# Attention of a two-layer trunk on one core: the turned weights and the values of two heads issued together, value columns of four heads in one matmul, and the lower parts of the first turned blocks in row order

## The chip, the cores and the metric

The kernel runs on one core of a Trainium2 chip. The metric is device time in microseconds. Three runs of the kernel before took 1935.15, 1935.57 and 1936.12 us; their median, 1935.57 us, is the time before. One more execution was profiled, and every row of a profile below is from such an execution.

## What is computed

A trunk of two layers over 256 rows of 2048 columns, all in float32. The first layer mixes rows with a convolution module, the second with latent attention over 16 heads; each is followed by a squared-ReLU MLP, and an RMS norm stands ahead of each part and at the end. What the change touches is the attention:

```python
down = h @ w_in
c_q, c_kv, k_pe = jnp.split(down, [Q_LORA_RANK, Q_LORA_RANK + KV_LORA_RANK], axis=-1)
q = (rms_norm(c_q, q_norm_g) @ w_q_up).reshape(B, S, N_HEADS, QK_NOPE_DIM + QK_ROPE_DIM)
...
kv = (rms_norm(c_kv, kv_norm_g) @ w_kv_up).reshape(B, S, N_HEADS, QK_NOPE_DIM + V_HEAD_DIM)
k_nope, v = jnp.split(kv, [QK_NOPE_DIM], axis=-1)
...
s = (jnp.einsum('bqhd,bkhd->bhqk', qn, k_nope)
     + jnp.einsum('bqhr,bkr->bhqk', qp, k_pe)).astype(jnp.float32) * scale
s = jnp.where(mask[None, None], s, -jnp.inf)
p = jax.nn.softmax(s, axis=-1).astype(v.dtype)
return jnp.einsum('bhqk,bkhd->bqhd', p, v)
...
return o @ w_o
```

The latent vectors have 512 columns; a head has 128 key columns, 64 rotary columns and 128 value columns. In the weight `w_kv_up` the 128 key columns and the 128 value columns of a head lie side by side, head after head.

## The kernel before

Products in float32 are made of two parts. A weight block comes in by DMA (`raw`, three buffers), ScalarE rounds it to its upper part (`hi`, line 169), VectorE subtracts to get the lower part (`lo`, line 173), six buffers of each. `mm3` (lines 202 to 204) then issues three matmuls for one product: upper by upper, lower by upper, upper by lower. The data side is split in the same way, by `hi_part` (208) and `lo_part` (213, or 215 with a scale). Only turns (transposes by an identity matrix) and the product of softmax weights and values run in plain float32; the trace lists a plain float32 matmul as two rows.

PSUM has eight banks. During the MLP all eight are `acc`; in the attention six are `acc` and two are `tr`, each kind used in rotation.

At the end of the first layer's MLP, `Sums.plain` calls `prepare` for the column blocks 0 and 1 of the new rows. Each `prepare` turns four 128-column blocks in two calls of `to_T`, two blocks to a PSUM bank. ScalarE takes the upper parts from the bank. VectorE's lower parts follow at once for the first call; for the second they are put in the list `rest`, which the next call with `rest` runs (or, at the end, the caller). The attention's first product reads these blocks, and its banks are those that the MLP gave up.

The attention works in groups of four heads (`HG = 4`). What a group needs is a list of pieces: `qp_piece` (rotary columns of a row half), `qn_piece` (a head's query, twelve matmuls of 256 columns), and `kv_piece`, eight to a group: for each pair of heads two pieces that make a head's keys (twelve matmuls of 256 columns) and two that make the values of both heads for a row half (line 1540 ff., again twelve matmuls, the moving operand being two runs of 128 value columns). The weight of a pair is one unit and one DMA of 1 MB (`kv_unit`). `start_unit` and `prefetch` start the split of the unit two places ahead and the load of the unit three further on. In the loop over heads the pieces of the group that comes next stand between the steps of the heads of this one; in the last group they are pieces of the output product (`o_piece`). One head runs:

```python
scores(h)
piece(todo.pop(0))
weights(h)
prefetch(1)
piece(todo.pop(0))
if h > 0:
    weights_turn(h - 1)
if i > 1 and g + 1 < NG:
    qp_turn(g + 1, i - 2)
if h > 1:
    values(h - 2)
```

`scores` makes ten matmuls into an `acc` bank, VectorE takes the row maxima (1640, 1641), ScalarE the exponentials (1643); `weights` divides by the sums on VectorE (1650, 1653) into `pr`. `weights_turn` turns the three 128 x 128 blocks of `pr` into a `tr` bank (1659) and ScalarE copies them to `pT` (1661). `qp_turn` turns the rotary parts of two heads of the next group into a `tr` bank (1597) and ScalarE copies them twice (1606, 1607). `values` multiplies `pT` with `vv` (1668, 1669) into an `acc` bank, which is split into `oh` and `ol` (208, 213). Everything from the down projection on is under `tc.manual_schedule()`: each engine runs its instructions in the order written. The number of pieces per head is 3, 2, 2, 2 in group 0, 4, 4, 3, 3 in groups 1 and 2, and 3 each in group 3.

Of the kernel before, what the change touches and what calls it, by code (L numbers as in the profile page):

```python
# [78 lines left out]
def trunk_kernel(  # L79
# [59 lines left out]
    def nm(s):  # L139
        uid[0] += 1  # L140
        return f"{s}_{uid[0]}"
# [233 lines left out]
    def residual_stage(last, gain, r_scale=None, raw=None, by_steps=()):  # L375
# [18 lines left out]
        def prepare(n, only=None, half=None, out=None, rest=None):  # L394
            sl = columns(n, half)
            if last:
                if n in by_steps:
                    step()
                    steps.extend(turn_block(n, gain, raw))
                elif gain is not None:  # L400
                    for j in range(2):
                        to_T(xs, 4 * n + 2 * j, xh, xl, gain, rest if j == 1 else None)
# [961 lines left out]
    with ExitStack() as cx:  # L1364
# [34 lines left out]
        def kv_unit(g, i):  # L1399
            unit(("kvu", g, i), [rows(mla_w_kv_up[0], 0, NJ, (g * HG + 2 * i) * (DN + DV), 2 * (DN + DV))],  # L1400
                 [P, NJ, 2 * (DN + DV)])
# [8 lines left out]
        for g in range(NG):  # L1410
            if g == 0:
                kv_unit(g, 0)
                kv_unit(g, 1)
                q_units(g)
            else:
                q_units(g)
                kv_unit(g, 0)
                kv_unit(g, 1)
# [90 lines left out]
        kTs, vvs, qTs, qps, qpAs = {}, {}, {}, {}, {}  # L1509
# [8 lines left out]
        def kv_piece(g, i, c):  # L1518

            key = ("kvu", g, i)  # L1520
            if i == 0 and c == 0:
                kTs[g] = parts_tile("kT")
                vvs[g] = gp[0].tile([P, T, HG * DV], F32, tag="vv", name=nm("vv"))
            if c % 2 == 0:
                start_unit(key, c // 2)
            po = acc_tile()
            if c < 2:
                o = po[:, :S]
                ns = slice(c * (DN + DV), c * (DN + DV) + DN)
                for j in range(NJ):  # L1530
                    wh, wl = w_at(key, j)
                    nc.tensor.matmul(o, wh[:, ns], kvh[:, j, :], start=j == 0, stop=False)  # L1532
                    nc.tensor.matmul(o, wh[:, ns], kvl[:, j, :], start=False, stop=False)  # L1533
                    nc.tensor.matmul(o, wl[:, ns], kvh[:, j, :], start=False, stop=j == NJ - 1)  # L1534
                in_parts(o, kTs[g], 2 * i + c)
            else:
                t = c - 2
                ts = slice(t * P, (t + 1) * P)
                o = po[:, : 2 * DV].rearrange("p (h n) -> p h n", h=2)
                for j in range(NJ):  # L1540
                    wh, wl = (a.rearrange("p (h n) -> p h n", h=2)[:, :, DN:] for a in w_at(key, j))
                    mm3(o, kvh[:, j, ts], kvl[:, j, ts], wh, wl, j == 0, j == NJ - 1)
                nc.vector.tensor_copy(vvs[g][:, t, 2 * i * DV : 2 * (i + 1) * DV], po[:, : 2 * DV])
# [65 lines left out]
        def kv_work(g):  # L1609
            return [lambda i=i, c=c: kv_piece(g, i, c) for i in range(HG // 2) for c in range(4)]  # L1610
# [14 lines left out]
        def scores(h):  # L1625
# [5 lines left out]
            pr = prs[h] = at2.tile([P, 3 * P], F32, tag="pr", name=nm("pr"))  # L1631
# [46 lines left out]
        def o_piece(k):  # L1678
# [5 lines left out]
            for b in range(2):  # L1684
                bs = slice(b * NB, (b + 1) * NB)
                for t in range(T):
                    mm3(ps_o[b][t], oh_kt(k, t), ol_kt(k, t), wh[:, bs], wl[:, bs], k == 0, k == H - 1)

        with tc.manual_schedule():
# [95 lines left out]
            for g in range(NG):  # L1785
                for i in range(HG):
# [11 lines left out]
                    if h > 0:  # L1798
                        weights_turn(h - 1)
                    if i > 1 and g + 1 < NG:  # L1800
                        qp_turn(g + 1, i - 2)
                    if h > 1:
                        values(h - 2)
# [115 lines left out]
```

## Time and profile before

| what | value |
|---|---|
| median of three runs (lowest to highest) | 1935.57 us (1935.15 to 1936.12) |
| profiled execution, its own time | 1935.27 us |
| its span in the trace | 1933.5 us |
| granted TensorE clock, mean over the span | 0.999 |
| PE, VectorE, ScalarE busy, share of the span | 99%, 82%, 57% |
| attention, first scores to last values | 1063.9 to 1191.2 us of the span |

A row of the timeline gives the start in us from the start of the span, the duration in us, engine, line of the kernel, operation, tiles as out<-in, shape, how many instructions were merged, and in brackets the idle time ahead of it with what ended it. Matmuls are pipelined: one starts before the one ahead of it has ended, so that the cost of one in a row of many is the distance between two starts, not the duration in its row. A row with "issue" or a releaser in brackets is where an engine stood still.

### The profile page before, as it was taken

The page shows a single profiled execution, that of the slowest core. Times are in us where ns is not written, and L with a number is a line of the kernel's source. Part 1 is how long each engine was busy: PE and PEld are TensorE (multiplying, and loading weights), DVE is VectorE, ACT ScalarE, POOL GpSimd, SP SyncE. Part 2 cuts the span into 40 slices and gives each one's busy share as a digit, 9 for nine tenths or more (in the row PEclk, how much of TensorE's full clock was granted, in tenths as well). Part 3 has the DMA queues.
Part 4 walks back from the last instruction along what each step waited for, and adds up shares of the span by engine and source line. Part 5 has one row for each costly group of instructions (what it writes and reads, how often), then busy time and mean ns, then how long its engine had stood idle before and what let it go on. Part 6 is the DMA issues. An engine that isn't in the chain of part 4 may idle for free.

```text
span 1933.5 us, 28599 instructions
## 1 busy us (share of the span) xinstructions
PE 1919.0 (99%) x10805; PEld 1684.2 (87%) x10805; DVE 1592.3 (82%) x2464; ACT 1095.5 (57%) x1634; POOL 249.0 (13%) x208
## 2 busy tenths in 40 slices
PE   8999999999999999999999999999999999999998
PEld 8999888888888888888899998888888888888886
DVE  7999988877989777799976766877789887678898
ACT  5667755554555555555586655555555554455554
POOL 6999200000010100000001420000000010000000
PEclk9999999999999999999999999999999999999999
DMA  7766456665585866555665445465546686665674
GB/s 230 214 184 188 153 192 205 192 195 176 177 253 190 262 199 186 192 174 196 218 188 161 142 133 191 157 217 185 187 163 224 214 251 219 191 196 175 231 220 148
DMA packets 217756, 375.50 MB, mean 194 GB/s; under 512 B 16009, under 2 KB 91025, under 8 KB 217361
## 3 DMA queue, kind: packets, MB, share of 16 engines
q1 hardware_dynamic: 211968, 363.28, 58.2%
q0 software_dynamic: 4320, 7.87, 2.2%
q10 hardware_dynamic: 1328, 2.52, 0.4%
q8 instruction: 84, 1.38, 0.3%
q14 instruction: 56, 0.45, 0.1%
HBM read 363.68 MB, written 2.10 MB: 189 GB/s over the span
## 4 chain that ended last, share of the span: by engine, by line
PE 96%; DVE 2%; issue 0%; DMA 0%; ACT 0%; ACTq 0%; DVEq 0%
PE acc L650 24%; PE acc L202 15%; PE acc L204 15%; PE acc L203 15%; PE acc L651 13%; PE acc L818 8%; PE acc L1281 2%; DVE sum L905 1%; DMA xs<-in_x 0%; PE acc L1532 0%; PE acc L1555 0%; PE acc L1557 0%; PE acc L1556 0%; PE acc L1534 0%; PE acc L1533 0%
## 5 line engine op out<-in xcount | busy, mean ns | idle before, releaser
L173 DVE TENSOR_TENSOR lo<-raw,hi 128x1024 fp32r<-128x1024 f32 (+2 forms) x509 | 601.7, 1197 | 231.6 <-ACT hi L169 227.8
L169 ACT ACTIVATE hi<-raw 128x1024 fp32r<-128x1024 f32 (+2 forms) x574 | 583.9, 1036 | 358.4 <-PE acc L650 196.6
L650 PE MATMUL acc<-xt,hi 128*128 128x512 f32 x2048 | 710.5, 390 | 0.0
L651 PE MATMUL acc<-xt,lo 128*128 128x256 f32 x2048 | 577.5, 282 | 0.0
L650 PEld LDWEIGHTS acc<-xt,hi 128*128 128x128 f32 x2048 | 384.4, 188 | 80.6
L651 PEld LDWEIGHTS acc<-xt,lo 128*128 128x128 f32 x2048 | 387.1, 189 | 0.2
L494 ACT ACTIVATE hi<-raw 128x1024 fp32r<-128x1024 f32 x248 | 228.8, 949 | 234.8 <-DVE raw L502 137.6
L495 DVE TENSOR_TENSOR lo<-raw,hi 128x1024 fp32r<-128x1024 f32 x248 | 264.0, 1087 | 31.9 <-ACT hi L494 27.9
L202 PE MATMUL acc<-hi,sh 128*128 128x512 f32 x514 | 200.1, 389 | 0.0
L204 PE MATMUL acc<-lo,sh 128*128 128x512 f32 x514 | 200.1, 389 | 0.0
L202 PE MATMUL acc<-hi,gh 128*128 128x512 f32 (+1 forms) x516 | 200.0, 388 | 0.0
L203 PE MATMUL acc<-hi,gl 128*128 128x512 f32 (+1 forms) x516 | 199.9, 387 | 0.0
L204 PE MATMUL acc<-lo,gh 128*128 128x512 f32 (+1 forms) x516 | 199.9, 387 | 0.0
L818 PE MATMUL acc<-xt,hi 128*128 128x256 f32 x1024 | 180.1, 281 | 0.3 <-ACT b L1100 0.2
L203 PE MATMUL acc<-hi,sl 128*128 128x512 f32 x450 | 175.1, 389 | 0.0
L575 POOL DMA_DIRECT2D xs<-v x30 | 26.4, 972 | 1138.2 <-DVE lo L173 703.9
L905 DVE SCALAR_TENSOR_TENSOR sum<-ub,w_dw,sum 128x256 f32<-128x256 f32 x409 | 164.4, 484 | 3.5 <-ACT sum L875 3.0
L173 POOL TENSOR_TENSOR lo<-raw,hi 128x1024 fp32r<-128x1024 f32 x65 | 155.1, 2410 | 17.3 <-ACT hi L169 17.3
L818 PEld LDWEIGHTS acc<-xt,hi 128*128 128x128 f32 x1024 | 154.5, 188 | 1.1 <-ACT xt L1084 0.6
L818 PE MATMUL acc<-xt,lo 128*128 128x256 f32 x512 | 139.2, 279 | 0.0
L204 PEld LDWEIGHTS acc<-lo,sh 128*128 128x128 f32 x514 | 96.5, 188 | 20.5 <-DVE lo L495 0.3
L204 PEld LDWEIGHTS acc<-lo,gh 128*128 128x128 f32 x516 | 96.9, 188 | 19.9
(311 smaller groups left out, 2563.1 us busy)
## 6 DMA issues: line engine op xcount, KB each, us to landing
raw<-in_mlp_w SPq DMA_DIRECT2D x255, 1024.0 KB, 5.4
raw<-in_conv_w_pw SPq DMA_DIRECT2D x62, 512.0 KB, 5.0
raw<-in_conv_w_pw SPq DMA_DIRECT2D x16, 1024.0 KB, 5.0
raw<-in_mla_w_o SPq DMA_DIRECT2D x16, 1024.0 KB, 5.3
raw<-in_mla_w_kv_up SPq DMA_DIRECT2D x8, 1024.0 KB, 5.3
xs<-v POOLq DMA_DIRECT2D x30, 256.0 KB, 7.7
raw<-in_mla_w_in SPq DMA_DIRECT2D x8, 576.0 KB, 4.6
raw<-in_mla_w_in SPq DMA_DIRECT2D x4, 1024.0 KB
```

The lines of the kernel that those rows point to most:

```text
L169: nc.scalar.activation(hi, raw[:, js, :], AF.Copy)
L173: eng.tensor_tensor(lo, raw, hi.bitcast(F32), op=ALU.subtract)
L202: nc.tensor.matmul(ps, sh, mh, start=start, stop=False)
L203: nc.tensor.matmul(ps, sl, mh, start=False, stop=False)
L204: nc.tensor.matmul(ps, sh, ml, start=False, stop=stop)
L494: nc.scalar.activation(hi, src, AF.Copy)
L495: nc.vector.tensor_tensor(lo, src, hi.bitcast(F32), op=ALU.subtract)
L650: nc.tensor.matmul(ps[b], wh[:, bs], xhl(k), start=k == 0, stop=False)
L651: nc.tensor.matmul(ps[b][:, :S], wl[:, bs], xh(k), start=False, stop=k == KC - 1)
L818: nc.tensor.matmul(pss[c][b][:, :S], w[i][:, bs], (xh, xl)[j](k), start=k == i + j == 0, stop=end and k == k0 + nk - 1 and (i, j) == terms ...
L905: nc.vector.scalar_tensor_tensor(out=out, in0=ubs[c][:, w : w + S], scalar=tap(c, w), in1=base, op0=ALU.mult, op1=ALU.add)
L1281: nc.tensor.matmul(ps2[b][t], x_kt(k, t), w[:, bs], start=k == g == i == 0, stop=k == KC - 1 and i == len(group) - 1,)
```

## The change

It has three parts.

1. `prepare`: before the first `to_T` of a column block, the list `rest` is emptied. The lower parts of blocks 2 and 3 then come ahead of those of 4 and 5. (Blocks are counted in 128 columns; this acts at one place, the end of the first MLP, since elsewhere `rest` is absent or empty.)
2. The units of `w_kv_up`: instead of two units of two heads with keys and values, a group has one unit with the key columns of four heads and one with the value columns of four heads. Each is loaded by four DMAs of 256 KB, in runs of 128 columns (512 bytes) where there were runs of 512 columns. A key piece is as before. A value piece now makes the values of four heads for a row half, with a moving operand of 512 columns; it is cut into two halves of six matmuls that add into one bank, and one copy of 512 columns ends it. A group has still eight pieces: four of keys, then four halves of values.
3. The order of turns and values: `plain_work` takes the place of the three calls in the loop. At an even head from 4 on it issues values(h - 4), weights_turn(h - 2), perhaps one qp_turn, values(h - 3), weights_turn(h - 1); at an odd head nothing, but for heads 1 and 15. `qp_turn(g, 1)` moves from the last head of a group to the first of the next. `pr` has a third buffer.

```diff
@@ prepare
                 elif gain is not None:
+                    while rest:
+                        rest.pop(0)()
                     for j in range(2):
                         to_T(xs, 4 * n + 2 * j, xh, xl, gain, rest if j == 1 else None)
@@ units
-        def kv_unit(g, i):
-            unit(("kvu", g, i), [rows(mla_w_kv_up[0], 0, NJ, (g * HG + 2 * i) * (DN + DV), 2 * (DN + DV))],
-                 [P, NJ, 2 * (DN + DV)])
+        wkv4 = mla_w_kv_up[0].rearrange("(j p) (h n) -> p j h n", p=P, n=DN + DV)
+
+        def kv_units(g):
+            hs = slice(g * HG, (g + 1) * HG)
+            for kind, ns in (("k", slice(0, DN)), ("v", slice(DN, DN + DV))):
+                unit((kind, g), [wkv4[:, j : j + 1, hs, ns] for j in range(NJ)], [P, NJ, HG * DN])
@@ pieces
+        def k_piece(g, i):
+            key = ("k", g)
...
+            if i % 2 == 0:
+                start_unit(key, i // 2)
+            o = acc_tile()[:, :S]
+            ns = slice(i * DN, (i + 1) * DN)
+            for j in range(NJ):
+                wh, wl = w_at(key, j)
+                nc.tensor.matmul(o, wh[:, ns], kvh[:, j, :], start=j == 0, stop=False)
+                nc.tensor.matmul(o, wh[:, ns], kvl[:, j, :], start=False, stop=False)
+                nc.tensor.matmul(o, wl[:, ns], kvh[:, j, :], start=False, stop=j == NJ - 1)
+            in_parts(o, kTs[g], i)
+
+        def v_piece(g, t, half):
+            key = ("v", g)
+            if half == 0:
+                start_unit(key, t)
+                vos[g, t] = acc_tile()
+            o, ts = vos[g, t], slice(t * P, (t + 1) * P)
+            for j in range(half * NJ // 2, (half + 1) * NJ // 2):
+                mm3(o, kvh[:, j, ts], kvl[:, j, ts], *w_at(key, j), j == 0, j == NJ - 1)
+            if half == 1:
+                if t == 0:
+                    vvs[g] = gp[0].tile([P, T, HG * DV], F32, tag="vv", name=nm("vv"))
+                nc.vector.tensor_copy(vvs[g][:, t, :], o)
@@ kv_work
-            return [lambda i=i, c=c: kv_piece(g, i, c) for i in range(HG // 2) for c in range(4)]
+            return [lambda i=i: k_piece(g, i) for i in range(HG)] + [
+                lambda t=t, half=half: v_piece(g, t, half) for t in range(T) for half in range(2)
+            ]
@@ scores
-            pr = prs[h] = at2.tile([P, 3 * P], F32, tag="pr", name=nm("pr"))
+            pr = prs[h] = at2.tile([P, 3 * P], F32, tag="pr", name=nm("pr"), bufs=3)
@@ new
+        def plain_work(h):
+            g, i = divmod(h, HG)
+            if h == H - 1:
+                values(h - 3)
+                weights_turn(h - 1)
+                values(h - 2)
+            elif h == 1:
+                weights_turn(0)
+            elif h % 2 == 0:
+                if h > 2:
+                    values(h - 4)
+                    weights_turn(h - 2)
+                if i == 2 and g + 1 < NG:
+                    qp_turn(g + 1, 0)
+                if i == 0 and g > 0:
+                    qp_turn(g, 1)
+                if h > 2:
+                    values(h - 3)
+                if h > 0:
+                    weights_turn(h - 1)
@@ loop over heads
-                    if h > 0:
-                        weights_turn(h - 1)
-                    if i > 1 and g + 1 < NG:
-                        qp_turn(g + 1, i - 2)
-                    if h > 1:
-                        values(h - 2)
+                    plain_work(h)
```

More of the change, by code (lines that the diff above doesn't have):

```diff
@@ L1411, in trunk_kernel @@
             if g == 0:
-                kv_unit(g, 0)
-                kv_unit(g, 1)
+                kv_units(g)
                 q_units(g)
@@ L1416, in trunk_kernel @@
                 q_units(g)
-                kv_unit(g, 0)
-                kv_unit(g, 1)
+                kv_units(g)
         for m in range(H // 2):
@@ L1506, in trunk_kernel @@
         gp = []
-        kTs, vvs, qTs, qps, qpAs = {}, {}, {}, {}, {}
+        kTs, vvs, vos, qTs, qps, qpAs = {}, {}, {}, {}, {}, {}
         def parts_tile(tag):
@@ L1516, in in_parts @@
             lo_part(o, parts[0][:, i, :], parts[1][:, i, :])
-        def kv_piece(g, i, c):
-            key = ("kvu", g, i)
-            if i == 0 and c == 0:
+        def k_piece(g, i):
+            key = ("k", g)
+            if i == 0:
                 kTs[g] = parts_tile("kT")
[L1523 to L1543, printed above, removed]
```

## The prediction

> **What bounds the kernel now.** I read the page from the top.
>
> ```profile
> span 1933.5 us, 28599 instructions
> PE 1919.0 (99%) x10805; PEld 1684.2 (87%) x10805; DVE 1592.3 (82%) x2464; ACT 1095.5 (57%) x1634; POOL 249.0 (13%) x208
> ...
> PEclk9999999999999999999999999999999999999999
> ...
> PE 96%; DVE 2%; issue 0%; DMA 0%; ACT 0%; ACTq 0%; DVEq 0%
> ```
>
> TensorE is the chain: 96% of it, at full granted clock in all forty slices. So an edit is worth what it takes from or adds to TensorE's own line of starts; the other engines count only where a matmul waits for them. In the waits of the attention (window 1000 to 1200 us) no row has PE waiting. The timeline of PE just before that window shows the one place near the change where it does, so I ask there and inside the head loop.
>
> **Part 1, the row order of the lower parts.** The timeline of PE and DVE where the first MLP ends:
>
> ```profile
> 983.66 0.39 PE L204 MATMUL acc<-lo,gh 128*128 128x512 f32 x1
> 984.43 0.38 PE L202 MATMUL acc<-hi,xt 128*128 128x288 f32 x1 [0.39 <-DVE xt L215]
> ...
> 982.24 2.44 DVE L215 SCALAR_TENSOR_TENSOR xt<-acc,vecs,xt 128x256 fp32r<-128x256 f32 x6
> 984.60 1.28 DVE L598 TENSOR_TENSOR xs<-acc,xs 128x512 f32<-128x512 f32 x2
> ...
> L215 DVE SCALAR_TENSOR_TENSOR xt<-tr,vecs,xt 128x256 fp32r<-128x256 f32 x24 | 10.1, 477 | 1.8 <-PE tr L266 1.8
> ```
>
> Six lower parts run in 2.44 us. With a last one of 0.48 us (477 ns is the mean of this shape in the group quoted last) they stand (2.44 - 0.48) / 5 = 0.39 us apart. The built program has them in the order of blocks 0, 1, 2, 4, 5, 3, and the attention's first matmul waits not for its data but for its bank, the one from which blocks 4 and 5 are taken: it is released by the lower part of block 5, the fifth, which ends at 982.24 + 4 x 0.39 + 0.48 = 984.28, and starts at 984.43. In row order block 5 is the sixth. So this edit lengthens the wait: **+0.39 us**. Nothing hides it. If the bank were not what it waits for, it would be 0; a gain is excluded, as block 0, which the data need, is first in both. The sums of line 598 behind the six keep their time, and so does the load of ScalarE.
>
> **Part 2, value columns of four heads at once.** Per group 48 matmuls of 256 columns become 24 of 512; over four groups 192 become 96. PE's timeline of head 3 to the first piece of head 5 gives the distance at 256; the two rows of line 202 with `oh` are the first and last of 29 matmuls of 512 (one in a row, output product), those with `xt` the first and last of 19 (query product):
>
> ```profile
> 1078.86 0.31 PE L202 MATMUL acc<-kTh,qTh 128*128 128x128 f32 x1
> 1080.09 0.28 PE L202 MATMUL acc<-hi,kvh 128*128 128x256 f32 x1
> 1082.93 0.49 PE L1659 MATMUL tr<-ident,pr 128*128 128x128 f32 x3
> 1083.26 0.60 PE L1597 MATMUL tr<-ident,qhl 128*128 128x128 f32 x4
> 1083.69 0.60 PE L1668 MATMUL acc<-pT,vv 128*128 128x256 f32 x2
> 1084.13 0.38 PE L1669 MATMUL acc<-pT,vv 128*128 128x128 f32 x2
> 1084.27 0.30 PE L202 MATMUL acc<-kTh,qTh 128*128 128x128 f32 x1
> 1088.35 0.49 PE L1659 MATMUL tr<-ident,pr 128*128 128x128 f32 x3
> 1088.67 0.60 PE L1668 MATMUL acc<-pT,vv 128*128 128x256 f32 x2
> 1089.25 0.36 PE L1555 MATMUL acc<-qh,hi 128*128 128x256 f32 x1
> 1089.45 0.28 PE L1556 MATMUL acc<-ql,hi 128*128 128x256 f32 x1
> ...
> 1208.19 0.39 PE L202 MATMUL acc<-hi,oh 128*128 128x512 f32 x1
> 1214.55 0.39 PE L203 MATMUL acc<-hi,ol 128*128 128x512 f32 x1
> ...
> 1011.65 0.40 PE L202 MATMUL acc<-hi,xt 128*128 128x512 f32 x1
> 1015.85 0.40 PE L202 MATMUL acc<-hi,xt 128*128 128x512 f32 x1
> ```
>
> From 1080.09 to 1082.93 lie two value pieces, 24 matmuls: 118.3 ns each. At 512 it is 6.36 / 28 = 227 ns or 4.20 / 18 = 233 ns. So 192 x 118.3 = 22.7 us become 96 x 227 = 21.8 or 96 x 233 = 22.4: a gain of 0.9 to 0.3 us. I take **-0.8 us**, near the `oh` rows, whose products stand in the same head loop. A form of 512 that costs two of 256 would give 0.
>
> By the Trainium skill ("TensorE: Matmul & The Clock Gate", section "Wait — 56ns, not 53.3ns?") a matmul costs its columns at 2.4 GHz and about 2.5 ns; halving the count would then save 96 x 2.5 ns = 0.24 us. The trace does not agree: beyond the columns at that clock its rows hold 11 to 20 ns per matmul.
>
> VectorE's copies of `vv` go from 16 of 256 columns to 8 of 512, and the split work has the same bytes; both lie beside matmuls. The loads change from one DMA to four per unit:
>
> ```profile
> raw<-in_mla_w_kv_up SPq DMA_DIRECT2D x8, 1024.0 KB, 5.3
> raw<-in_mla_w_q_up SPq DMA_DIRECT2D x16, 256.0 KB, 3.4
> ...
> 1065.88 2.02 SPq L1432 DMA_DIRECT2D raw<-in_mla_w_q_up  x4
> ...
> ACT hi L169 <- DMA raw<-in_mla_w_in: 2.0, 2, 1.0
> ```
>
> The query units are loaded in just this form, 4 x 256 KB in runs of 512 bytes: four issues in 2.02 us, so that the last one lands some 1.5 + 3.4 = 4.9 us after the first issue, against 5.3. SP's queue holds 1.6 us more per unit, eight times; behind it stands only the next load, some 5 us later. In the same window the only splits that waited for a DMA are two of `mla_w_in`, before the heads. So 0, hidden by loads that run two units ahead; without that cover, the 1.6 us of each issue, 8 x 1.6 = 12.8.
>
> The Trainium skill ("DMA: Bandwidth & Descriptors", section "Bandwidth") asks for batches of 1 MiB for three quarters of the peak rate. By it the key and value loads would get slower; the row of 3.4 us for a quarter shows that the cost per load is there, and the waits that it has not been felt.
>
> **Part 3, turns and values in pairs.** Plain float32 work stands in 17 stretches now (heads 1 to 15, two at the end), 11 after. One stretch costs little beyond its matmuls: the first product after it shows 0.20 us to the next start (1089.25 to 1089.45) for 0.118, and most of this is the last value rows running out. I take 0.02 us each, -0.1 us; by the whole 0.08 it would be -0.5.
>
> What weighs is a new wait. At heads 4, 6, 8, 10 and 12 a stretch is now values, turn, rotary turn, values, turn: three `tr` tiles, and there are two banks. In the built program the last turn waits for ScalarE's copy `pT` of the first. From the rows above, a turn takes 0.33 us, the rotary turn 0.43, the values 0.58, so the third tile is due 0.58 + 0.33 + 0.43 + 0.58 = 1.92 us after the stretch begins. Ahead of that copy ScalarE has everything of the head. DVE and ACT around head 4:
>
> ```profile
> 1081.93 0.61 DVE L1640 TENSOR_REDUCE mx<-acc 128x1 f32<-128x128 f32 x2
> 1086.34 0.42 DVE L213 TENSOR_TENSOR ol<-acc,oh 128x256 fp32r<-128x256 f32 x1
> 1086.68 0.61 DVE L1640 TENSOR_REDUCE mx<-acc 128x1 f32<-128x128 f32 x2
> ...
> 1087.59 0.37 ACT L1643 ACTIVATE pr<-acc,mx 128x128 f32<-128x128 f32 x1 [1.29 <-DVE mx L1641]
> 1088.66 1.06 ACT L169 ACTIVATE hi<-raw 128x1024 fp32r<-128x1024 f32 x1
> 1089.88 0.51 ACT L1661 ACTIVATE pT<-tr 128x384 f32<-128x384 f32 x1
> 1090.25 0.41 ACT L208 ACTIVATE oh<-acc 128x256 fp32r<-128x256 f32 x1
> ```
>
> PE first. Head 3 loses its stretch (1082.93 to 1084.27, 1.34 us) and 0.1 us of its pieces: head 4's scores follow head 3's after 5.41 - 1.44 = 3.97 us. Its stretch begins 4.08 us later (1084.27 to 1088.35), the third tile is due 1.92 after that: 1078.86 + 9.97 = 1088.83.
>
> Now the copy. VectorE takes the maxima of head 4 at 1086.68, not because the scores are late but because its queue is: head 3's were taken at 1081.93, and between lie 4.75 us of exponentials waited for, a split, two copies of `vv` and an `ol`. Without the `ol` (0.34 us to the next start), with a wider copy, it is about 4.6, and the `ol` that is gone ahead of head 3 too brings all of it some 0.5 earlier (its 0.34 and a wait for its `oh`, which I guess): maxima at 1086.0 to 1086.6. From there to ScalarE's turn for the copy are 1089.88 - 1086.68 = 3.20 us (maxima, exponentials, query parts, a split of 1.06). Then `oh` (0.37) and the copy (0.51): 1090.1 to 1090.7. The third tile waits 1.3 to 1.9 us, more if the skipped values at head 2 bring PE forward by another 0.58. I take 1.8 us.
>
> At head 8 ScalarE reached its copy late as well, at the others at once or almost:
>
> ```profile
> 1117.48 0.49 PE L1659 MATMUL tr<-ident,pr 128*128 128x128 f32 x3
> ...
> 1118.74 0.51 ACT L1661 ACTIVATE pT<-tr 128x384 f32<-128x384 f32 x1
> ...
> ACT pT L1661 <- PE tr L1659: 12.0, 5, 3.1
> ```
>
> There the copy would end at 1118.74 + 0.37 + 0.51 = 1119.62 against 1117.48 + 1.92 = 1119.40. Five of sixteen copies found ScalarE idle. For heads 6, 8, 10 and 12 I take 0.4 us together; the least is 0, the most head 4's 1.8 at each. Together **+2.2 us**. Behind the waiting turn stands PE's whole queue, so the wait goes to the end; the later scores are late by as much, which lets VectorE catch up. The values themselves come two heads after their weights, and the output product reads heads 0 to 11 as before or later than written: no wait.
>
> **Sum**: +0.39 - 0.8 - 0.1 + 2.2 = +1.7 us. The profiled execution took 1935.27 us, 1.77 beside its span; it becomes 1937.0. It lies 0.3 us under the median of the runs, so against that: **1937.3 us**.
>
> **Rivals.** (a) The copies come in time: VectorE, with less to do in heads 1 to 3, catches up, and the third tile is free. For it: VectorE is 82% busy over the span, and five copies found ScalarE idle. Against it: the backlog of head 4. Then +0.39 - 0.8 - 0.1 = -0.5, 1935.1, not slower. (b) The backlog is in every stretch of three: two heads' turns, copies and splits come at once, and ScalarE starts each five-part stretch behind. Price: 1.8 at five places, +0.39 - 0.9 + 9.0 = +8.5, 1944; it is over the bound below once the waits exceed 4.4 us in all. For it: PE reaches every even head earlier by a missing stretch of about 1.1 to 1.3 us. Against it: in groups 1 and 2 heads have three or four pieces, in group 3 long ones, so the queues drain. (c) The quartered loads land late by SP's 1.6 us each: +12.8 - 0.5, 1947.6; the waits and the 4.9 us speak against it. (d) The change does not do what it says: a 512-column matmul costs two of 256; the forecast goes up by 0.8 and stays in its range.
>
> **How the numbers follow.** What a measurement can tell from no change is about 0.2%, 3.9 us: faster is below 1931.7, slower above 1939.4. Forecast 0.53 (from -0.3 to +3.8 by its bounds, so 1935.3 to 1939.4), rival (a) 0.22, (b) 0.17, (c) 0.04, and 0.04 for a gain that I have no row for. (d) lies inside the first. Within 0.2%: 0.53 + 0.22 = 0.75; slower: 0.17 + 0.04 = 0.21; faster: 0.04. The range 1934.7 to 1939.8 takes in the forecast, (a), and the low end of (b).
>
> **What would show it.** Part 1: PE idle ahead of its first matmul of the attention 0.8 us, not 0.39. Part 2: `vv` pieces with starts 227 to 233 ns apart. Part 3: rows of PE waiting for ACT `pT` at line 1666, longest at head 4. Loads: no split waiting for `in_mla_w_kv_up`. Wrong would be the forecast if no such row is there, if it stands at all five heads with over 1 us, or if PE waits in the heads for anything else.

## The result, and the profile after

The changed kernel takes 1938.26 us (median of 22 runs, 1937.64 to 1939.75) where the kernel before, beside it on the same chip, takes 1935.2 us (22 runs, 1935.0 to 1936.37): a ratio of 1.0015, 95% interval 1.0008 to 1.0022. That is 3.06 us slower, 0.16%, and within the 0.2% that the prediction called no change. In a later session it took 1938.23 us (11 runs) beside 1935.77 us for the kernel before, ratio 1.0016 (1.0007 to 1.0025).

The page of the changed kernel, its profiled execution at 1939.75 us:

```profile
span 1938.0 us, 28442 instructions
PE 1920.3 (99%) x10709; PEld 1680.8 (87%) x10709; DVE 1591.0 (82%) x2456; ACT 1094.2 (56%) x1634; POOL 248.9 (13%) x208
...
PE 95%; DVE 3%; ACT 1%; DMA 1%; issue 0%; ACTq 0%; SPq 0%; DVEq 0%
...
raw<-in_mla_w_kv_up SPq DMA_DIRECT2D x32, 256.0 KB, 4.3
```

TensorE has 96 matmuls fewer and is still the chain. One per cent of this span is 19 us, so the shares of the chain are too coarse to say where 3 us went. To find that out I took the same five matmuls in every trace and compared the distances between them. They are, in the kernel before, the last `L204 acc<-lo,gh` of the first feed-forward (983.66), the first `L202 acc<-hi,xt` of the attention (984.43), the last `L204 acc<-lo,oh` (1241.97), the first `L650 acc<-xt,hi` of the second feed-forward (1242.20) and the last matmul of all (1925.32). What lies ahead of the first of them is code that no version touches; the profiled execution of the changed kernel lost 1.15 us there, which is not the change. A distance runs from the start of one of them to the start of the next. The table gives them in us, and in brackets what a kernel adds to the kernel before (experiments e1 to e12 follow below):

| kernel | 1: into the attention | 2: attention | 3: into the second feed-forward | 4: to the end |
|---|---|---|---|---|
| before | 0.77 | 257.54 | 0.23 | 683.12 |
| changed | 0.96 (+0.19) | 259.64 (+2.10) | 0.59 (+0.36) | 683.90 (+0.78) |
| changed, again (e12) | 0.94 (+0.17) | 259.73 (+2.19) | 0.58 (+0.35) | 683.51 (+0.39) |
| e1 row order alone | 1.10 (+0.33) | 257.55 (0) | 0.23 (0) | 683.21 (+0.09) |
| e2 columns alone | 0.63 (-0.14) | 257.13 (-0.41) | 0.59 (+0.36) | 684.02 (+0.90) |
| e3 pairs alone | 0.60 (-0.17) | 258.92 (+1.38) | 0.23 (0) | 683.56 (+0.44) |
| e4 changed less row order | 0.71 (-0.06) | 259.65 (+2.11) | 0.59 (+0.36) | 683.84 (+0.72) |
| e5 bank order mended | 1.14 (+0.37) | 259.69 (+2.15) | 0.23 (0) | 683.10 (-0.02) |
| e6 two turns in acc | 1.12 (+0.35) | 258.68 (+1.14) | 0.22 (0) | 683.35 (+0.23) |
| e7 rotary turns apart | 1.12 (+0.35) | 259.57 (+2.03) | 0.58 (+0.35) | 683.17 (+0.05) |
| e8 value copy on ScalarE | 1.15 (+0.38) | 258.48 (+0.94) | 0.58 (+0.35) | 683.28 (+0.16) |
| e9 four third turns in acc | 0.97 (+0.20) | 257.23 (-0.31) | 0.23 (0) | 683.07 (-0.05) |
| e10 columns, banks mended | 0.68 (-0.09) | 257.13 (-0.41) | 0.22 (0) | 683.07 (-0.05) |
| e11 combined | 0.73 (-0.04) | 257.25 (-0.29) | 0.22 (0) | 683.83 (+0.71) |

So the time went to four places: a little into distance 1, most into the attention, some at the first matmul behind it, and some near the end. In the profiles below, rows between those shown are left out.

**Into the attention.** The timelines of PE, DVE and ACT of the changed kernel there:

```profile
984.81 0.39 PE L204 MATMUL acc<-lo,gh 128*128 128x512 f32 x1
985.77 0.37 PE L202 MATMUL acc<-hi,xt 128*128 128x288 f32 x1 [0.57 <-ACT hi L169]
...
983.19 2.43 DVE L215 SCALAR_TENSOR_TENSOR xt<-acc,vecs,xt 128x256 fp32r<-128x256 f32 x6
...
984.33 1.37 ACT L169 ACTIVATE hi<-raw 128x576 fp32r<-128x576 f32 x2
```

The six lower parts end at 985.62 and the matmul starts 0.15 us later. The releaser named is a split on ScalarE that ends at 985.70; e1 below tells the two apart.

**The value columns.** The first and the last of the twelve matmuls of the first two half pieces with 512 columns, on PE's timeline, and the group of the copies that end such pieces:

```profile
1042.31 0.39 PE L202 MATMUL acc<-hi,kvh 128*128 128x512 f32 x1
1044.87 0.40 PE L204 MATMUL acc<-lo,kvh 128*128 128x512 f32 x1
...
L1548 DVE COPY vv<-acc x8: 683/684/692, 1045.3 to 1144.6; 128x512 f32<-128x512 f32 x8
```

2.56 us over 11 steps is 232.7 ns each: the `xt` price of the prediction, not the `oh` price. The copy takes 684 ns.

**The third turn.** PE, DVE and ACT in head 4 of the changed kernel:

```profile
1087.44 0.59 PE L1675 MATMUL acc<-pT,vv 128*128 128x256 f32 x2
1088.09 0.49 PE L1666 MATMUL tr<-ident,pr 128*128 128x128 f32 x3
1088.41 0.60 PE L1602 MATMUL tr<-ident,qhl 128*128 128x128 f32 x4
1089.29 0.38 PE L1676 MATMUL acc<-pT,vv 128*128 128x128 f32 x2
1091.47 0.55 PE L1666 MATMUL tr<-ident,pr 128*128 128x128 f32 x3 [1.80 <-ACT pT L1668]
...
1085.71 1.23 DVE L173 TENSOR_TENSOR lo<-raw,hi 128x1024 fp32r<-128x1024 f32 x1 [0.20 <-ACT hi L169]
1086.85 0.68 DVE L1548 COPY vv<-acc 128x512 f32<-128x512 f32 x1
1087.45 0.61 DVE L1647 TENSOR_REDUCE mx<-acc 128x1 f32<-128x128 f32 x2
...
1088.36 0.37 ACT L1650 ACTIVATE pr<-acc,mx 128x128 f32<-128x128 f32 x1 [2.69 <-DVE mx L1648]
1089.43 1.06 ACT L169 ACTIVATE hi<-raw 128x1024 fp32r<-128x1024 f32 x1
1090.64 0.40 ACT L208 ACTIVATE oh<-acc 128x256 fp32r<-128x256 f32 x1
1090.91 0.51 ACT L1668 ACTIVATE pT<-tr 128x384 f32<-128x384 f32 x1
```

The two turn banks are taken by the first turn (1088.09) and the rotary turn (1088.41). Read on from the end: the third turn starts at 1091.47, 0.05 us after ScalarE's copy of the first turn ended (1090.91 + 0.51 = 1091.42), though that first turn was done at 1088.09 + 0.49. ScalarE is late because its exponentials waited 2.69 us for the maxima, and VectorE took these behind a split and the value copy. In the waits (window 1000 to 1200 us) of the same kernel:

```profile
PE tr L1666 <- ACT pT L1668: 2.1, 2, 1.8
DVE lo L173 <- DMA raw<-in_mla_w_q_up: 1.8, 1, 1.8
DVE lo L173 <- DMA raw<-in_mla_w_kv_up: 0.9, 1, 0.9
```

Two waits (1.80 at head 4, 0.33 at head 10) are all that PE has there. Against the usual 0.11 us from the last value matmul to the next turn they cost 1.97 and 0.49 us in TensorE's order, that is, in how much later its next matmul starts; 2.46 together. Two splits on VectorE wait for transfers, one of them for `in_mla_w_kv_up`, which no split of the kernel before did; no matmul waits for those splits.

**Into the second feed-forward.** PE and DVE of the changed kernel:

```profile
1245.41 0.39 PE L204 MATMUL acc<-lo,oh 128*128 128x512 f32 x1
1246.00 0.47 PE L652 MATMUL acc<-xt,hi 128*128 128x512 f32 x1 [0.20 <-DVE xs L387]
...
1245.16 1.37 DVE L387 TENSOR_TENSOR xs<-acc,xs 128x512 f32<-128x512 f32 x2
```

The first `L652` does not need what `L387` computes. It waits until the first of two additions has read its accumulator. In the built programs the feed-forward opens in accumulator bank 0; the attention's last accumulators stand in banks 3 and 1 before, and in 0 and 2 after, because the attention takes 24 accumulators for its key and value pieces where it took 32, and the six banks are handed out in turn.

**Near the end.** The one row of PE with a wait between 1500 and 1900 us in the changed kernel:

```profile
1897.55 0.50 PE L204 MATMUL acc<-lo,sh 128*128 128x512 f32 x1 [0.44 <-DVE lo L497]
```

A split weight of the second feed-forward is late; the kernel before has no such row. The matmul that waits is the one that starts at 1893.09 us in the kernel before.

### The profile page after: what moved, and what is told of

Same layout as the page of the kernel before. It is cut to its first block, busy times and chain, and to the rows that moved or that the text cites. A ratio compares the mean times of both kernels' runs of the same rounds, so it can differ in the third digit from the quotient of the medians.

```text
span 1938.0 us, 28442 instructions
## 1 busy us (share of the span) xinstructions
PE 1920.3 (99%) x10709; PEld 1680.8 (87%) x10709; DVE 1591.0 (82%) x2456; ACT 1094.2 (56%) x1634; POOL 248.9 (13%) x208
## 3 DMA queue, kind: packets, MB, share of 16 engines
q8 instruction: 84, 1.38, 0.3%
## 4 chain that ended last, share of the span: by engine, by line
PE 95%; DVE 3%; ACT 1%; DMA 1%; issue 0%; ACTq 0%; SPq 0%; DVEq 0%
PE acc L652 24%; PE acc L204 15%; PE acc L202 15%; PE acc L203 15%; PE acc L653 13%; PE acc L820 8%; PE acc L1283 2%; DVE sum L907 1%; ACT hi L169 0%; DMA xs<-in_x 0%; PE tr L266 0%; DVE lo L173 0%; PE acc L1560 0%; PE acc L1561 0%; PE acc L1562 0%
## 5 line engine op out<-in xcount | busy, mean ns | idle before, releaser
L652 PE MATMUL acc<-xt,hi 128*128 128x512 f32 x2048 | 710.6, 390 | 0.2 <-DVE xs L387 0.2
L652 PEld LDWEIGHTS acc<-xt,hi 128*128 128x128 f32 x2048 | 384.5, 188 | 81.1 <-issue 0.6
L204 PE MATMUL acc<-lo,sh 128*128 128x512 f32 x514 | 200.2, 390 | 0.4 <-DVE lo L497 0.4
L202 PE MATMUL acc<-hi,sh 128*128 128x512 f32 x514 | 200.2, 389 | 0.0
L202 PE MATMUL acc<-hi,gh 128*128 128x512 f32 (+1 forms) x516 | 200.0, 388 | 0.0
L204 PE MATMUL acc<-lo,gh 128*128 128x512 f32 (+1 forms) x516 | 199.9, 387 | 0.0
L204 PEld LDWEIGHTS acc<-lo,sh 128*128 128x128 f32 x514 | 96.5, 188 | 21.2 <-DVE lo L497 1.2
L204 PEld LDWEIGHTS acc<-lo,gh 128*128 128x128 f32 x516 | 96.9, 188 | 19.8
```

The source lines that it names most:

```text
L202: nc.tensor.matmul(ps, sh, mh, start=start, stop=False)
L204: nc.tensor.matmul(ps, sh, ml, start=False, stop=stop)
L652: nc.tensor.matmul(ps[b], wh[:, bs], xhl(k), start=k == 0, stop=False)
```

## The experiments

All were run in five rounds beside the kernel before; each median stands with that of the kernel before in the same session.

**e1, row order alone.** The kernel before, with

```
                 elif gain is not None:
+                    while rest:
+                        rest.pop(0)()
                     for j in range(2):
```

> The kernel before with the first part alone (lower parts of blocks 4 and 5 in row order ahead of their first turns). Theory: the first L204 xt matmul of the attention takes its accumulator bank behind a lower part of block 5, the sixth of the six L215 in place of the fifth, so one more of 0.39 us lies on TensorE's path: +0.2 to +0.4 us in TensorE's order at that place (0.18 was read in the profile of the changed kernel) and as much at the end, 1935.4 to 1935.6 where the kernel before is at 1935.2. Rival, that VectorE makes it up before the next time TensorE waits for it: 0. A gain in the rows behind (the first L202 to L204 xt matmuls waiting less for the lower parts of block 4): under 0.

1935.73 against 1935.53 us, ratio 1.0002 (0.9993 to 1.0011). PE, DVE and ACT of e1:

```profile
984.83 0.37 PE L202 MATMUL acc<-hi,xt 128*128 128x288 f32 x1 [0.71 <-DVE xt L215]
...
982.25 2.43 DVE L215 SCALAR_TENSOR_TENSOR xt<-acc,vecs,xt 128x256 fp32r<-128x256 f32 x6
...
983.24 1.37 ACT L169 ACTIVATE hi<-raw 128x576 fp32r<-128x576 f32 x2
```

The six lower parts stand where they stood in the kernel before (982.25 against 982.24), ScalarE's second split ends at 984.61, before the last of them, and the matmul starts 0.40 us later than before: 0.15 us after the end of the sixth (984.68), where before it started 0.14 us after the end of the fifth (984.29). This holds in every trace: with the edit 0.14 to 0.15 us behind the sixth (changed, e1, e5 to e9, e12), without it 0.14 to 0.15 us behind the fifth (before, e2 to e4, e10, e11). Distance 1 also depends on how far VectorE was ahead of TensorE in that execution; but it is 0.94 to 1.15 us in the eight traces with the edit and 0.60 to 0.77 in the six without it, and the two means, 1.06 and 0.69, are about 0.38 us apart. The time itself, +0.20 us, is too small to be told from none.

**e2, columns alone.** The kernel before with the units `("k", g)` and `("v", g)`, `k_piece`, `v_piece` and the new `kv_work`; the loop over heads as before.

> The kernel before with the second part alone (keys and values in units of their own, value matmuls of 512 columns). Theory of the prediction: 96 matmuls of 227 us/1000 in place of 192 of 118.3 us/1000, -0.9 us; by the 232 to 235 us/1000 that the changed kernel's profile shows: 96 x (2 x 118.3 - 233) = -0.3 us. Theory of the bank order: eight accumulator tiles fewer shift the banks by two, and the second feed-forward's first matmul takes a bank that the last additions of the attention still read, +0.4 us at its start, so the end is within 0.2 us of the kernel before. Rival, late transfers: a wait of TensorE on L173's splits, +1 us or more each, +12 us if each group has one.

1935.64 against 1935.53 us, ratio 1.0 (0.9991 to 1.0009). TensorE comes out of the attention 0.41 us ahead and loses 0.36 us at the first matmul behind it: the lower of the two prices (-0.3) and the theory of the bank order hold, the -0.9 does not, and in the attention no wait for a transfer reaches TensorE. Distance 4 then adds 0.90 us in this profile, of which more below.

**e3, pairs alone.** The kernel before with `plain_work(h)` in the loop over heads and `bufs=3` for `pr`.

> The kernel before with the third part alone (turns and values of two heads together, three buffers of pr). Theory of the third turn: at heads 4 and 10 TensorE waits about 1.8 to 2.0 and 0.3 to 0.5 us for the copy that frees a turn's bank, 2.1 to 2.5 us in all, and +0.4 us or nothing at the other even heads; fewer plain stretches give back 0.1 us: +2.0 to +2.4 us at the end. Rival, that the wait is an effect of the value pieces (their place in the work list) and not of the pairing: no wait of over 0.3 us at L1666, and 0 us at the end.

1936.73 against 1935.53 us, ratio 1.0006 (0.9997 to 1.0015). The wait is there without the new value pieces, so the pairing makes it; but it is 1.01 us long at head 4 (1.17 in TensorE's order), and the other delay, 0.21 in TensorE's order, is at head 8 and not at head 10: 1.38 us where the changed kernel has 2.46. PE of e3 at heads 4 and 8, DVE between heads 3 and 4, and ACT at heads 3, 4 and 8:

```profile
1088.01 0.38 PE L1669 MATMUL acc<-pT,vv 128*128 128x128 f32 x2
1089.41 0.55 PE L1659 MATMUL tr<-ident,pr 128*128 128x128 f32 x3 [1.01 <-ACT pT L1661]
1118.81 0.55 PE L1659 MATMUL tr<-ident,pr 128*128 128x128 f32 x3
...
1085.06 0.42 DVE L1543 COPY vv<-acc 128x256 f32<-128x256 f32 x1
1085.39 0.61 DVE L1640 TENSOR_REDUCE mx<-acc 128x1 f32<-128x128 f32 x2
...
1082.02 0.37 ACT L1643 ACTIVATE pr<-acc,mx 128x128 f32<-128x128 f32 x1 [0.87 <-DVE mx L1641]
1086.30 0.37 ACT L1643 ACTIVATE pr<-acc,mx 128x128 f32<-128x128 f32 x1 [2.42 <-DVE mx L1641]
1118.24 0.52 ACT L1661 ACTIVATE pT<-tr 128x384 f32<-128x384 f32 x1
```

At head 8 the third turn starts 0.05 us after the copy's end (1118.76), too short a gap to be shown in brackets. From the exponentials of head 3 to those of head 4 there are 4.28 us. They go round a loop: exponentials, the upper part of a split on ScalarE, its lower part on VectorE, the value copy, the maxima, exponentials. The copy of 256 columns takes 0.42 us in it.

**e4, the changed kernel without the row order** (its two added lines taken out).

> The changed kernel without its first part. Theory: the sixth L215 is off TensorE's path, -0.2 to -0.4 us against the changed kernel, so +2.7 to +2.9 us against the kernel before where the changed one is at +3.06. Rival, that the parts do not add (the delay at the first attention matmul is taken up by a later wait): the same +3.06.

1937.71 against 1935.53 us, ratio 1.0012 (1.0003 to 1.002). +2.18, less than the +2.7 to +2.9 expected; against the changed kernel distance 1 is shorter by 0.25 us, and its attention is the same (+2.11). The same two rows of ACT:

```profile
1082.61 0.37 ACT L1648 ACTIVATE pr<-acc,mx 128x128 f32<-128x128 f32 x1 [1.36 <-DVE mx L1646]
1087.15 0.37 ACT L1648 ACTIVATE pr<-acc,mx 128x128 f32<-128x128 f32 x1 [2.68 <-DVE mx L1646]
```

Here the loop takes 4.54 us: longer by 0.26, which is the copy of 512 columns (0.68 for 0.42). The parts do not add: the columns alone give 0.41 us and the pairs alone cost 1.38, but together they cost 2.11 in the attention, not 0.97, because the third turn's waits grow. At head 4 the cost is 0.8 us more than in e3. TensorE comes 0.16 us earlier, and ScalarE's copy of the first turn ends 0.64 us later, both counted from the first matmul of the attention. The wider copy in the loop explains 0.26 of that. Another 0.41 us is there already at the exponentials of head 2 (93.50 us after that matmul, 93.09 in e3), and e8 below, without the copy on VectorE, has it too (93.51). ScalarE has two key parts (`kTh`) between heads 1 and 2 where e3 has none, since the keys of four heads now come first; that this makes the 0.41 us is not shown, as no run changes that order alone.

**e5, four accumulators more**, taken once ahead of head 0 in the changed kernel, so that the bank order at the second feed-forward is another.

```
             warm(AF.Exp)
+            for _ in range(4):
+                nc.vector.memset(acc_tile()[:, 0:1], 0.0)
             for w in work[:3]:
```

> The changed kernel with four accumulator tiles more (a one-column memset each on VectorE, ahead of the last pieces before head 0), so that the attention's last accumulators do not stand in the banks that the second feed-forward opens with. Theory of the bank order: the first L652 of the second feed-forward no longer waits for the last additions L387; TensorE's order of the changed kernel loses the 0.36 us that it gained at that place, all else as it is: -0.3 to -0.4 us, +2.7 against the kernel before. Rival, that the wait there is for another thing (the split weights of the feed-forward) and only changes its name: 0.

1937.63 against 1935.15 us, ratio 1.0012 (1.0004 to 1.0021): +2.48. PE and DVE of e5:

```profile
1244.35 0.39 PE L204 MATMUL acc<-lo,oh 128*128 128x512 f32 x1
1244.58 0.40 PE L652 MATMUL acc<-xt,hi 128*128 128x512 f32 x1
...
1244.10 1.37 DVE L387 TENSOR_TENSOR xs<-acc,xs 128x512 f32<-128x512 f32 x2
```

The additions stand where they stood against TensorE (0.25 us ahead of its last matmul, as in the changed kernel), and the next matmul now starts 0.23 us behind the last one, without a wait. So it was the bank.

**e6, the third turn of heads 4 and 10 in an accumulator tile**, and two accumulators more ahead of head 0.

```
-                    weights_turn(h - 1)
+                    weights_turn(h - 1, acc_tile if h in (4, 10) else tr_tile)
```

> The changed kernel with the third turn of heads 4 and 10 in an accumulator tile instead of a turn tile, and two accumulator tiles more ahead of head 0 (as in e5, for the bank order of the feed-forward). Theory of the third turn: both waits of L1666 for L1668 go (1.80 and 0.33 us of waiting, 2.46 in TensorE's order), and the 0.36 us at the feed-forward go as well: -2.8 us against the changed kernel, +0.2 against the kernel before. Rival 1, that TensorE then waits as long for VectorE or ScalarE further on (the value matmul L1675 for the copy pT, the next scores for a bank): under half of it comes back, -1.2 us or less. Rival 2, that the wait is not for the bank: 0 at the turns.

1936.63 against 1935.15 us, ratio 1.0007 (0.9998 to 1.0017). Rival 1 comes nearest, though not at the places that it names: both waits are gone, but of their 2.46 us the attention keeps only 0.96 as a gain on the changed kernel, since 1.55 us are lost anew in TensorE's order at a place that had no wait before, the third turn of head 6. PE and ACT of e6:

```profile
1103.79 0.38 PE L1676 MATMUL acc<-pT,vv 128*128 128x128 f32 x2
1105.55 0.55 PE L1666 MATMUL tr<-ident,pr 128*128 128x128 f32 x3 [1.38 <-ACT pT L1668]
...
1104.98 0.51 ACT L1668 ACTIVATE pT<-tr 128x384 f32<-128x384 f32 x1
```

In the changed kernel TensorE reached head 6 some 2 us later and found the copy done.

**e7, rotary turns apart.** In `plain_work` both turns of a group at its fourth head, alone.

```
+            elif i == 3:
+                for m in range(2):
+                    qp_turn(g + 1, m)
             elif h % 2 == 0:
...
-                if i == 2 and g + 1 < NG:
-                    qp_turn(g + 1, 0)
-                if i == 0 and g > 0:
-                    qp_turn(g, 1)
```

> The changed kernel with the turns of the rotary queries taken out of the even heads: both of a group at its fourth head (3, 7, 11), alone, so that no stretch has more than two turns of weights. Theory of the third turn: no wait of over 0.2 us at L1666, -2.46 us, and three stretches of plain-f32 work more at 0.03 to 0.1 us each; the 0.36 us at the feed-forward stays: -2.1 to -2.4 against the changed kernel, +0.7 to +1.0 against the kernel before. Rival, that the delay sits in the backlog of ScalarE and VectorE and shows at the next wait (scores of heads 4, 8, 12 for the copies qpA, qpB, now close ahead of them): less than half of it comes back.

The rival holds. PE and ACT of e7 at the scores of head 4:

```profile
1082.90 0.27 PE L204 MATMUL acc<-kTl,qTh 128*128 128x128 f32 x1
1085.06 0.33 PE L1644 MATMUL acc<-kpA,qpA 128*128 128x128 f32 x1 [1.89 <-ACT qpA L1611]
...
1084.42 0.59 ACT L1611 ACTIVATE qpA<-tr 128x512 fp32r<-128x512 f32 x1
```

No third turn waits; the scores of head 4 do, for 1.89 us, for a copy that stands behind the exponentials of head 3. The attention keeps +2.03 us. The median is 1939.44 against 1935.15 us, ratio 1.0021 (1.0012 to 1.003), but its eleven runs spread from 1937.55 to 1942.5 as no other kernel's did; the profiled one took 1937.77, 2.62 us over the kernel before, where its four distances add 2.78; what the rest of the spread comes from is open.

**e8, the value copy on ScalarE** in the changed kernel.

```
-                nc.vector.tensor_copy(vvs[g][:, t, :], o)
+                nc.scalar.activation(vvs[g][:, t, :], o, AF.Copy)
```

> The changed kernel with the copy of the values out of PSUM on ScalarE instead of VectorE. Theory of the loop: between two heads the maximum waits on VectorE behind the split L173 and the value copy (0.68 us in the changed kernel, 0.42 in e3), the exponentials wait for the maximum, the next split's upper part for the exponentials; without the copy each head's maximum comes 0.68 us sooner, twice ahead of head 4, so the wait of 1.80 us at the third turn of head 4 falls to 0.4 to 0.8, that of head 10 goes: -1.2 to -1.9 us against the changed kernel. Rival, that the copy (about 0.6 us) stands as long in ScalarE's order ahead of the exponentials: 0 us, or longer waits.

1937.13 against 1935.15 us, ratio 1.001 (1.0001 to 1.0019). PE, DVE and ACT of e8:

```profile
1089.67 0.55 PE L1666 MATMUL tr<-ident,pr 128*128 128x128 f32 x3 [0.63 <-ACT pT L1668]
...
1084.50 1.23 DVE L173 TENSOR_TENSOR lo<-raw,hi 128x1024 fp32r<-128x1024 f32 x1 [0.19 <-ACT hi L169]
1085.64 0.62 DVE L1647 TENSOR_REDUCE mx<-acc 128x1 f32<-128x128 f32 x2
...
1084.36 0.59 ACT L1548 ACTIVATE vv<-acc 128x512 f32<-128x512 f32 x1
```

The maxima follow the split at once, the copy falls into a time in which ScalarE waits anyway, the loop from head 3's exponentials to head 4's takes 3.95 us (4.55 in the changed kernel), and head 4's wait shrinks from 1.80 to 0.63 us, as the loop says. Head 10's stays at 0.33 us, against the expectation; so its cause is not the copy, and stays open.

**e9, four third turns in accumulator tiles**: as e6, at heads 4, 6, 8 and 10; head 12, which had no wait, keeps its turn tile.

```
-                    weights_turn(h - 1, acc_tile if h in (4, 10) else tr_tile)
+                    weights_turn(h - 1, acc_tile if 2 < h < 12 else tr_tile)
```

> As e6, but with the third turn of heads 4, 6, 8 and 10 in an accumulator tile (four accumulator tiles more ahead of head 0 for the bank order of the feed-forward). Theory of the bank: TensorE waits at L1666 only because a third turn stands in the bank of the first, so the 1.38 us that e6 waited at head 6 go too: -1.5 us against e6, 0 to -0.2 us against the kernel before. Theory of the backlog: what TensorE needs from ScalarE (copies pT, qpA, behind the exponentials) is as late as ever, and a wait of 1 us or more stands at the next instruction that reads one of them (L1675 for pT, L1644 for qpA): +1.0 to +1.6 us against the kernel before.

1935.85 against 1935.77 us, ratio 1.0001 (0.9992 to 1.001). The attention takes 0.31 us less than before, and its waits have no row of PE. Head 4 of e9, PE and ACT:

```profile
1088.27 0.39 PE L1676 MATMUL acc<-pT,vv 128*128 128x128 f32 x2
1088.49 0.49 PE L1666 MATMUL acc<-ident,pr 128*128 128x128 f32 x3
...
1089.75 0.52 ACT L1668 ACTIVATE pT<-tr 128x384 f32<-128x384 f32 x1
```

ScalarE makes its copy as late as ever, 1.26 us after the third turn has started; but nothing else needs that copy so soon. This decides between the theories: ScalarE's lateness is real (e7 shows what happens where a matmul reads it early), and in the changed kernel it reaches TensorE only through the shared bank.

**e10, columns alone, with the bank order mended** (e2 and two accumulators more ahead of head 0).

> The kernel before with the second part alone (as e2) and two accumulator tiles more ahead of head 0. e2's trace shows TensorE 0.41 us ahead of the kernel before at the last output projection of the attention, and that lost again at the second feed-forward's first bank. Theory of the bank order: the 0.4 us stay won, -0.3 to -0.4 us against the kernel before. Rival, that another wait takes them in the feed-forward (its weight splits on VectorE are close behind TensorE): 0 to -0.1 us.

1934.75 against 1935.77 us, ratio 0.9997 (0.9988 to 1.0005). In the trace the 0.41 us stay won to the end (-0.55 us over distances 1 to 4). In time it is the fastest version run and still cannot be told from the kernel before.

**e11, combined**: the changed kernel without the row order, with e8's copy and e9's turns, bank order mended.

> The changed kernel without its first part, with the third turns of heads 4 to 10 in accumulator tiles (as e9), the value copy on ScalarE (as e8) and the bank order of the feed-forward mended. Theory of the bank: nothing of the waits is left, 96 columns matmuls give 0.3 to 0.4 us, the first part's 0.35 us is gone: -0.4 to -0.6 us against the kernel before. Theory of the backlog: the value copy on ScalarE takes the 0.68 us per head out of the loop, and what e9 still waits falls to under 0.5 us: 0 to +0.4 us.

1935.74 against 1935.77 us, ratio 1.0002 (0.9993 to 1.0011). The attention has no wait and gains 0.29 us, no more than e9, and the -0.4 to -0.6 us of the first theory are not reached: with the bank free the shorter loop is worth nothing. The rest of its profile is late weights near the end (+0.71: 0.4 at the matmul named above, 0.3 some 22 us later).

**e12, the changed kernel again.**

> The changed kernel once more, beside the others on this chip. Waits of 1.8 and 0.3 us at the third turns of heads 4 and 10 and of 0.2 us (0.36 in TensorE's order) at the second feed-forward's first bank, as before. The late weights near 1893 us (0.6 us in TensorE's order in its first profile), if they come from where this program's transfers fall: again there, +3.1 us against the kernel before; if from one run to the next: not there in this profile, and +2.7 us, with runs of both kinds among the eleven.

1938.23 against 1935.77 us, +2.46, under both expected times. Distances 1 to 3 come back within 0.1 us. The late weight does not come back where it was: in this profile it is at 1539 us and worth 0.39. Over all profiles it falls on one of two matmuls, at 1893.09 and at 1536.01 us in the kernel before: on the first in the changed kernel, e2 and e11, on the second in e3, e4, e6 and e12 and with 0.12 us in e8, and on neither in the rest. Since one program shows it at two places, it is not fixed by the program; what moves it stays open.

## Why the prediction was right or wrong

The forecast of no measurable change with a small loss was right, 1937.3 us against 1938.26, with the right main cause; the loss was +1.7 us by forecast and +3.06 and +2.46 in the two sessions. Its steps:

- **Row order, +0.39.** Right in mechanism and size: the bank freed by the lower part of block 5, sixth instead of fifth, 0.40 us in e1. In the changed kernel's own profiles 0.17 to 0.19 of it show, as VectorE was 0.2 us further ahead there. The wait that was to show it, 0.8 us, reads 0.71 in e1 and 0.57 in the changed kernel.
- **Columns, -0.8.** Right in sign, mis-sized: 0.41 us in e2 and e10. The step that was wrong is the choice of the `oh` price, 227 ns, because those products stand in the same head loop; the rows have 232.7 ns, which gives 96 x (2 x 118.3 - 232.7) = 0.37 us. The low bound of the prediction (0.3) was the better value. The estimate by the rule of the Trainium skill ("TensorE: Matmul & The Clock Gate", section "Wait — 56ns, not 53.3ns?") was 0.24, nearer than my 0.8; but its 2.5 ns per matmul is not what these rows hold beyond their columns at 2.4 GHz: 11.6 ns at 256 and 19.4 ns at 512.
- **Loads, 0.** Right in value: no matmul waits for a transfer, and e2's attention shows the full gain. But the sign given for it, no split waiting for `in_mla_w_kv_up`, did not hold: one waits 0.9 us in the changed kernel and in e2, none in e3, which loads as before. The quarter loads took 4.3 us from issue to landing, not the 3.4 us that was taken over from the query units.
- **Fewer stretches, -0.1.** Not seen: e3's attention adds 1.38 us, which is just its two waits (1.17 + 0.21), and e9's gain (0.31) is smaller than that of the columns alone (0.41).
- **The third turn, +2.2.** Right in mechanism and place: the wait of `L1666` for `L1668`, longest at head 4. Predicted 1.8 there and 0.4 at the other four, measured 1.97 at head 4, 0.49 at head 10 and nothing at 6, 8 and 12. Head 8, which the prediction had singled out, had its delay (0.21, as read from the rows) in e3 alone. The copy ended at 1091.42; less the 1.34 us that this profile was late at the first attention matmul, 1090.08, against 1090.1 to 1090.7 predicted. TensorE was due at 1089.29 + 2 x 0.11 = 1089.51, so 1088.17 against 1088.83 predicted: it came 0.66 us early. Most of that is the 0.58 us of skipped values at head 2, which the prediction named and left out of its value. The 1.8 us put the copy's end at 1088.83 + 1.8 = 1090.63, 0.55 us later than it was. So the close value is in part luck: two errors of 0.66 and 0.55 us nearly cancel. So is the sum: the 0.4 us for the other heads came all at one of them, for a cause that is open.
- **What it missed.** The sum had no term for the bank order: eight accumulators fewer moved the attention's last ones into the bank that the second feed-forward opens with, +0.36 us (e5). With the measured terms, 0.18 + 2.46 - 0.41 + 0.36 = +2.6 us; e5, which is without the last term, is at +2.48 by median and +2.50 by its four distances. The medians of the changed kernel lie 0.5 us above this sum in one session (+3.06) and 0.1 below it in the other (+2.46). The late weight in distance 4, which comes and goes, is of that size; that it makes this difference is not shown.
- **The rivals.** (a), that the copies come in time, fell: the two waits are there. (b), a backlog at all five stretches, fell in the changed kernel, but had a point: when e6 took the waits at heads 4 and 10 away, head 6 had one of 1.38 us. TensorE's own delay at head 4 was what kept the later stretches free. (c) and (d) fell (e2), (d) narrowly: 232.7 ns against 2 x 118.3 = 236.6.

## What to carry to other kernels

When work of two steps is put together, count the buffers that the joined stretch holds at once, and ask what else stands in the queue of the engine that frees the first: here one turn bank too few cost 2.46 us, and accumulator banks in its place cured it (e9), while moving the turns elsewhere only moved the wait (e7). An edit that changes how many buffers a stage takes from a rotating pool changes which buffer every later stage meets: list them in the built program up to the next stage. And price each part together with the others: the wider copy and the new order of pieces that came with the gain in columns made the pairs wait longer (2.46 us against 1.38).

## What the runs showed of the hardware

A matmul of 512 columns costs 232.7 ns with `kvh` as its fixed operand, 233 with `xt` and 227 with `oh`, without a wait between them; no run here tells why. A released accumulator bank is taken 0.14 to 0.15 us after the end of the VectorE instruction that frees it, the same in all fourteen traces compared in e1. A turn bank is taken 0.05 us after the end of ScalarE's copy out of it (the changed kernel at head 4, e3 at head 8).
